# Down projection of a decoder layer: first operands in memory of their own, products 1, 6, 7 and 4 in one set of open banks, x brought into the result by transfers

## The chip, the cores and the metric

The kernel runs on one core of a Trainium2 chip. The metric is the device time of one execution in microseconds (us); lower is better. Inputs come from the chip's main memory and the result goes back there; on-chip work uses a large on-chip memory of 128 partitions, and a small accumulator memory of eight banks, each 128 x 512 float32, into which TensorE (PE) writes. VectorE (DVE) and ScalarE (ACT) do the elementwise work, GpSimd (POOL) a little, SyncE (SP) starts transfers (DMAs). Each engine works through its own list of instructions in order, and waits at an instruction until what it needs is there. A DMA that is started from an engine's list stands in that list like any other instruction.

## The reference

One decoder layer on 1024 tokens of width 1024: a SwiGLU feed-forward part, a token mixer (windowed attention and a gated delta rule), a second feed-forward part, a final norm. The change lies in the last matrix product of both feed-forward parts, the one with `w_down` (2816 x 1024).

```python
def swiglu(x, w_gate, w_up, w_down):
    return (jax.nn.silu(x @ w_gate) * (x @ w_up)) @ w_down

def reference(x, ...):
    for layer in range(DEPTH):           # DEPTH is 1
        x = x + 0.5 * swiglu(rmsnorm(x, ffn1_norm[layer]),
                             ffn1_w_gate[layer], ffn1_w_up[layer], ffn1_w_down[layer])
        h = rmsnorm(x, mix_norm[layer])
        x = x + hybrid_mixer(h, pos, w_in[layer], ...)
        x = x + 0.5 * swiglu(rmsnorm(x, ffn2_norm[layer]),
                             ffn2_w_gate[layer], ffn2_w_up[layer], ffn2_w_down[layer])
    return rmsnorm(x, final_norm)
```

## The kernel before

Float32 products are made from rounded halves. An operand v is split into H, which is v rounded (a CAST on ACT), and L = v - H (a subtraction on DVE); a product is the sum of three matmuls, H·H, L·H and H·L. Splitting one 128 x 512 block is therefore one ACT and one DVE instruction.

Both feed-forward parts use a 2 x 2 block scheme with seven block products in place of eight. The hidden part (`ff_hidden`, `ff_pair`) makes the activations for a pair of 128-wide blocks of the hidden width at a time, eleven pairs in all, and writes to memory, for each pair, seven combinations of them: the arrays `hd[0]` to `hd[6]` (in `order` rows `hd0_10` is `hd[0]` of pair 10). The write is `ff_left` (L259): a DMA that ACT starts. Three of the seven are activations themselves; the other four are sums that DVE makes in `ff_sums` (L264 to L271) at the end of a pair, each followed by its write. The tiles they are made in are called `e`; 14 of them take turns.

The down projection is `ff_down` (L451). It runs seven block products in the order 1, 5, 6, 7, 4, 3, 2. Each product n has eleven steps p, one for each pair: the left operand is `hd[n-1][p]`, loaded into a staging tile `st` (L461, seven tiles take turns) and split into `lH`, `lL`; the right operand is a block of `w_down`, or a combination of its blocks that DVE makes (tile `T`; two of the blocks are kept in the tiles `room`), and is split into `rH`, `rL`. A step then has 12 matmuls (L517): three for each of four banks. So a product has 132 matmuls. All loads are started by SP, in the order in which the program asks for them. The splits of the first two steps of product 1 (`head`) stand ahead of everything else of the projection.

The result is gathered in `acc` (1024 x 1024, in on-chip memory), in four quarters of four blocks each. Product 1 is in all four of them. Before the change, product 1 goes into the banks X, ACT writes half of it to the first quarter of `acc` (L531), x is loaded into eight tiles `xt` of 512 KB each (five take turns), and DVE makes the four starts "half of product 1 plus x" with 16 additions (L539 to L542). Product 5 is summed in other banks, Y; then X is opened anew for product 6, into which 7 and 4 are summed too. `add` (L524) adds half of a bank to a quarter of `acc`, one scalar_tensor_tensor on DVE for each block (L526).

The lines that matter:

```python
    X = [psum(C, tag) for tag in ("mm", "mm", "tC", "tC")]
    product(1, X, True)
    for t in range(4):
        nc.scalar.mul(quarter(0, 0, t), X[t], 0.5)
...
        tt(out=quarter(1, 1, t), in0=p1, in1=xs[0][:, 512:], op=ALU.add)
...
    product(5, Y, True)
    add(1, 1, Y)
    X = [psum(C, tag) for tag in ("mm", "mm", "tC", "tC")]
    product(6, X, True)
```

Memory is handed out in pools; a tile of the projection that lies where a tile of the hidden part lay must wait for the last use of that one. The order of instructions on each engine is set when the program is built, by a scheduler that goes by its own estimate of times.

Of the kernel before, what the change touches and what calls it, by code (L numbers as in the profile page):

```python
# [9 lines left out]
F32 = mybir.dt.float32  # L10
F32R = mybir.dt.float32r
I32 = mybir.dt.int32
AF = mybir.ActivationFunctionType
ALU = mybir.AluOpType
AX = mybir.AxisListType

P = 128
T = 1024
D = 1024
DFF = 2816  # L20
KT = D // P
NT = T // P
# [12 lines left out]
NPAIR = NF // 2  # L35
# [34 lines left out]
def psum(C, tag):  # L70
    return C.pp.tile([P, 512], F32, name=tag, tag=tag, bufs=BANKS[tag])
# [29 lines left out]
def rsqrt_cols(C, ssq, scale, eps, n, tag, pool=None):  # L101

    nc = C.nc
    pool = pool or C.tp
    v = pool.tile([P, n], F32, name=tag + "v", tag=tag + "v", bufs=4)
    y = pool.tile([P, n], F32, name=tag + "y", tag=tag + "y", bufs=4)
    t = pool.tile([P, n], F32, name=tag + "t", tag=tag + "t", bufs=4)
    nc.vector.tensor_scalar(v, ssq, scale, eps, op0=ALU.mult, op1=ALU.add)
    yi = y.bitcast(I32)
    nc.vector.tensor_scalar(yi, v.bitcast(I32), 1, -1, op0=ALU.logical_shift_right, op1=ALU.bitwise_xor)  # L110
    nc.vector.tensor_tensor(out=yi, in0=yi, in1=C.magic[:, :n], op=ALU.add)
    for _ in range(3):
        nc.vector.tensor_tensor(out=t, in0=y, in1=y, op=ALU.mult)
        nc.vector.scalar_tensor_tensor(t, t, -0.5, v, op0=ALU.mult, op1=ALU.mult)
        nc.vector.scalar_tensor_tensor(y, t, 1.5, y, op0=ALU.add, op1=ALU.mult)
    return y, v
# [136 lines left out]


def ff_e(C):
    return C.ep.tile([P, 512], F32, name="e", tag="e", bufs=14)


def ff_left(C, n, p, v):  # L259

    C.nc.scalar.dma_start(C.hd[n - 1][p], v)


def ff_sums(C, p, a11, a12, a21, a22):  # L264

    tt = C.nc.vector.tensor_tensor
    S = [ff_e(C) for _ in range(4)]
    tt(out=S[2], in0=a11, in1=a21, op=ALU.subtract)
    tt(out=S[0], in0=a21, in1=a22, op=ALU.add)
    tt(out=S[1], in0=S[0], in1=a11, op=ALU.subtract)  # L270
    tt(out=S[3], in0=a12, in1=S[1], op=ALU.subtract)  # L271
    for n, v in ((7, S[2]), (5, S[0]), (6, S[1]), (3, S[3])):
        ff_left(C, n, p, v)


def ff_plain(C, W, a, n=512):

    nc = C.nc
    acc = [(psum(C, "mm"), psum(C, "tC")) for _ in W]
    for n0 in range(0, 512, n):  # L280
        for wpair, pair in zip(W, acc):
            for halves, ps in zip(wpair, pair):
                c = slice(a * 512 + n0, a * 512 + n0 + n)
                for k in range(KT):
                    H, L = [v[:, k % 4 * P:k % 4 * P + P] for v in halves[k // 4]]
                    for i, (x, w) in enumerate(((C.hH, H), (C.hL, H), (C.hH, L))):
                        nc.tensor.matmul(ps[:, n0:n0 + n], w, x[:, k, c], start=k == 0 and i == 0, stop=k == KT - 1 and i == 2)  # L287
    out = []
    for pg, pu in acc:
        sg = ff_e(C)  # L290
        nc.scalar.activation(sg, pg, AF.Silu)
        nc.vector.tensor_tensor(out=sg, in0=sg, in1=pu, op=ALU.mult)
        out.append(sg)
    return out
# [156 lines left out]
def ff_down(C, x_dram, wd, early, late, between=None):  # L451

    nc = C.nc
    tt = nc.vector.tensor_tensor
    lead = []

    def stage(src):
        v = C.fp.tile([P, 512], F32, name="st", tag="st", bufs=7)[:, :src.shape[1]]  # L460
        lead.append(nc.sync.dma_start(v, src).ins)  # L461
        return v

    def load(v, src):
        with C.tc.issue_after(lead[11]):
            nc.sync.dma_start(v, src)

    def split(v, tag, bufs):
        out = [C.fp.tile([P, 512], F32R, name=tag + nm, tag=tag + nm, bufs=bufs) for nm in "HL"]
        n = v.shape[1]  # L470
        H, L = [o[:, :n] for o in out]
        nc.scalar.copy(H, v)  # L472
        tt(out=L, in0=v, in1=H.bitcast(F32), op=ALU.subtract)  # L473
        return H, L

    def block(p, k, c):
        r = (2 * p + k) * P
        return wd[r:r + P, c * 512:c * 512 + 512]


    B12, B22 = [C.hp.tile([P, 16, 512], F32, name="room", tag=nm, bufs=1) for nm in ("hH", "hL")]
    head = [(split(stage(C.hd[0][p]), "l", 6), split(stage(block(p, 0, 0)), "r", 8)) for p in range(2)]
    acc = C.fp.tile([P, NT, D], F32, name="acc")
    T = C.w0.tile([P, NPAIR, 512], F32, name="T", tag="T", bufs=1)
    T = [T[:, p] for p in range(NPAIR)]
    B12, B22 = [[b[:, p] for p in range(NPAIR)] for b in (B12, B22)]

    def right(n, p):
        if n == 1:
            return split(stage(block(p, 0, 0)), "r", 8)  # L490
        if n == 5:
            load(B12[p], block(p, 0, 1))
            tt(out=T[p], in0=B12[p], in1=stage(block(p, 0, 0)), op=ALU.subtract)
        elif n == 6:
            load(B22[p], block(p, 1, 1))
            tt(out=T[p], in0=B22[p], in1=T[p], op=ALU.subtract)
        elif n == 7:
            v = C.fp.tile([P, 512], F32, name="st", tag="st", bufs=7)
            tt(out=v, in0=B22[p], in1=B12[p], op=ALU.subtract)
            return split(v, "r", 8)  # L500
        elif n == 4:
            tt(out=T[p], in0=stage(block(p, 1, 0)), in1=T[p], op=ALU.subtract)
        v = (B22[p] if n == 3 else T[p]) if n != 2 else stage(block(p, 1, 0))
        return split(v, "r", 8)

    def product(n, banks, opens, ts=range(4)):
        c0, c1 = ts[0] * P, ts[-1] * P + P
        for p in range(NPAIR):
            if n == 1 and p < len(head):
                x, W = head[p]  # L510
            else:
                W = right(n, p)
                x = split(stage(C.hd[n - 1][p][:, c0:c1]), "l", 6)
            for t, ps in zip(ts, banks):
                m = slice(t * P - c0, t * P - c0 + P)
                for i, (a, b) in enumerate(((0, 0), (0, 1), (1, 0))):
                    nc.tensor.matmul(ps, x[a][:, m], W[b], start=opens and p == 0 and i == 0,  # L517
                                     stop=p == NPAIR - 1 and i == 2, skip_group_check=True)

    def quarter(r, c, t):  # L520
        return acc[:, r * 4 + t, c * 512:c * 512 + 512]

    def add(r, c, banks, ts=range(4)):
        for t, ps in zip(ts, banks):  # L524
            q = quarter(r, c, t)
            nc.vector.scalar_tensor_tensor(q, ps, 0.5, q, op0=ALU.mult, op1=ALU.add)  # L526

    X = [psum(C, tag) for tag in ("mm", "mm", "tC", "tC")]
    product(1, X, True)
    for t in range(4):  # L530
        nc.scalar.mul(quarter(0, 0, t), X[t], 0.5)  # L531
    for t in range(4):
        xs = []
        for r in (1, 0):
            xt = C.fp.tile([P, D], F32, name="xt", tag="xg", bufs=5)
            nc.sync.dma_start(xt, x_dram[(r * 4 + t) * P:(r * 4 + t) * P + P])
            xs.append(xt)
        p1 = quarter(0, 0, t)
        tt(out=quarter(1, 1, t), in0=p1, in1=xs[0][:, 512:], op=ALU.add)  # L539
        tt(out=quarter(1, 0, t), in0=p1, in1=xs[0][:, :512], op=ALU.add)  # L540
        tt(out=quarter(0, 1, t), in0=p1, in1=xs[1][:, 512:], op=ALU.add)
        tt(out=p1, in0=p1, in1=xs[1][:, :512], op=ALU.add)  # L542
    Y = [psum(C, tag) for tag in ("tA", "tA", "tM", "tM")]
    product(5, Y, True)
    add(1, 1, Y)
    X = [psum(C, tag) for tag in ("mm", "mm", "tC", "tC")]
    product(6, X, True)
    add(0, 1, X)
    product(7, X, False)
    add(1, 1, X)  # L550
    product(4, X, False)
    add(1, 0, X)
    product(3, Y, False)
    add(0, 1, Y)
    take_h(C)
    if between is not None:
        between()
    for t in range(4, 8):
        late([early(t, acc[:, t])])
    first = [early(t, acc[:, t]) for t in range(4)]  # L560
    for ts, tag in (((0, 1), "mm"), ((2, 3), "tC")):
        X = [psum(C, tag) for _ in ts]
        product(2, X, True, ts)
        add(0, 0, X, ts)
        late([first[t] for t in ts])


def consts(C, I):
# [939 lines left out]
def take_h(C):  # L1508
    C.hH, C.hL = [C.hp.tile([P, KT, T], F32R, name=nm, tag=nm, bufs=1) for nm in ("hH", "hL")]
# [118 lines left out]
```

## Time and profile before

| what | us |
|---|---|
| median of 3 runs | 2587.6 |
| lowest and highest of them | 2586.91, 2592.05 |
| the profiled execution, its own time | 2586.69 |
| its span in the profile | 2585.0 |
| first down projection in the span | about 462 to 690 |
| second down projection in the span | about 2351 to 2585 |

The profile gives each instruction's start and duration, and for an engine's idle time the event that ended it. Matmuls overlap: one that is listed with 0.39 us is followed by the next after about 0.23 us, so that times between starts, not durations, tell how long a row of them took. "PEclk" is the share of full speed that TensorE was granted.

### The profile page before, as it was taken

How to read it: one execution, taken by the hardware profiler on the slowest of the kernel's cores; microseconds unless marked ns; L12 is line 12 of the kernel's file. 1: busy time of each engine (PE TensorE's matmuls, PEld its weight loads, DVE VectorE, ACT ScalarE, POOL GpSimd, SP SyncE). 2: the span in 40 equal slices, each digit the busy share in tenths (PEclk: the TensorE clock that was granted, in tenths of full speed). 3: DMA queues.
4: the chain of work that ended last, by engine and by line, in shares of the span. 5: the costliest groups of instructions: out<-in, count | busy, mean ns of one | idle time of the engine just before them, and what ended most of it. 6: DMA issues, size and time to landing. Idle time of an engine off the chain costs nothing.

```text
span 2585.0 us, 35524 instructions
## 1 busy us (share of the span) xinstructions
PE 2504.2 (97%) x12835; PEld 2085.1 (81%) x12835; DVE 1756.3 (68%) x4032; ACT 1042.7 (40%) x1900; POOL 97.3 (4%) x96
## 2 busy tenths in 40 slices
PE   7899999899999999999999999999998999999998
PEld 7788888688888877888888888887877888887786
DVE  6966665697634447688887777356557766665977
ACT  4433332355533346444434343254343333333445
POOL 0000000000110010000000000001010000000000
PEclk9999999999999999999999999999999999999999
DMA  4233232765533332222223223265431323325656
GB/s 156 82 106 110 90 106 90 276 226 163 175 85 84 94 77 71 67 71 76 65 65 88 56 64 92 72 214 181 155 131 57 118 90 106 110 91 211 231 150 193
DMA packets 272176, 306.74 MB, mean 119 GB/s; under 512 B 43040, under 2 KB 188160, under 8 KB 272000
## 3 DMA queue, kind: packets, MB, share of 16 engines
q1 hardware_dynamic: 249824, 264.10, 32.9%
q10 hardware_dynamic: 22176, 40.38, 4.2%
q8 instruction: 101, 1.65, 0.3%
q14 instruction: 75, 0.61, 0.1%
HBM read 224.09 MB, written 74.02 MB: 115 GB/s over the span
## 4 chain that ended last, share of the span: by engine, by line
PE 87%; DVE 5%; DMA 4%; ACT 2%; issue 1%; SPq 0%; ACTq 0%; DVEq 0%
PE mm L82 28%; PE tC L388 12%; PE mm L388 8%; PE tM L388 8%; PE mm L517 6%; PE tC L517 5%; PE tC L82 4%; PE tA L82 2%; PE tA L517 2%; PE tM L517 2%; PE mm L287 2%; PE tC L287 2%; PE tM L82 1%; PE tA L86 1%; PE tC L1496 1%; DMA sgl<-sgbd 1%
## 5 line engine op out<-in xcount | busy, mean ns | idle before, releaser
L82 PE MATMUL mm<-hH,wL 128*128 128x512 f32 x960 | 384.9, 401 | 0.0
L82 PE MATMUL mm<-hH,wH 128*128 128x512 f32 x960 | 383.6, 400 | 0.0
L82 PE MATMUL mm<-hL,wH 128*128 128x512 f32 x960 | 380.9, 397 | 0.0
L236 ACT CAST fH<-fraw 128x512 fp32r<-128x512 f32 x256 | 156.0, 620 | 383.9 <-PE tC L388 68.6
L237 DVE TENSOR_TENSOR fL<-fraw,fH 128x512 fp32r<-128x512 f32 x256 | 173.5, 685 | 72.4 <-ACT fH L236 71.2
L82 PEld LDWEIGHTS mm<-hL,wH 128*128 128x128 f32 x960 | 181.1, 189 | 34.9
L82 PEld LDWEIGHTS mm<-hH,wL 128*128 128x128 f32 x960 | 180.9, 188 | 34.8
L82 PEld LDWEIGHTS mm<-hH,wH 128*128 128x128 f32 x960 | 181.1, 189 | 32.8
L472 ACT CAST lH<-st 128x512 fp32r<-128x512 f32 (+1 forms) x176 | 99.6, 566 | 153.4 <-issue 64.5
L133 DVE TENSOR_TENSOR wL<-wraw,wH 128x1024 fp32r<-128x1024 f32 x94 | 116.6, 1240 | 64.1 <-ACT wH L132 63.8
L473 DVE TENSOR_TENSOR lL<-st,lH 128x512 fp32r<-128x512 f32 (+1 forms) x176 | 113.1, 643 | 50.1 <-ACT lH L472 47.2
L132 ACT CAST wH<-wraw 128x1024 fp32r<-128x1024 f32 x94 | 98.4, 1049 | 115.6 <-PE mm L82 63.7
L388 PE MATMUL mm<-hH,fH 128*128 128x512 f32 x320 | 125.2, 391 | 0.0
L388 PE MATMUL mm<-hL,fH 128*128 128x512 f32 x320 | 125.0, 391 | 0.0
L388 PE MATMUL mm<-hH,fL 128*128 128x512 f32 x320 | 124.8, 390 | 0.0
L790 DVE CUSTOM_DVE_ANT_0 s<-tC,masks 128x128 f32<-128x128 f32 (+1 forms) x96 | 30.1, 348 | 103.0 <-PE tC L82 68.9
L517 PE MATMUL mm<-rH,lH 128*128 128x512 f32 x220 | 87.3, 397 | 12.0 <-ACT rH L472 12.0
L517 PE MATMUL mm<-rL,lH 128*128 128x512 f32 x220 | 87.5, 398 | 0.0
L517 PE MATMUL mm<-rH,lL 128*128 128x512 f32 x220 | 86.7, 394 | 0.0
L517 PE MATMUL tC<-rH,lH 128*128 128x512 f32 x220 | 86.4, 393 | 0.0
L517 PE MATMUL tC<-rH,lL 128*128 128x512 f32 x220 | 86.4, 393 | 0.0
L517 PE MATMUL tC<-rL,lH 128*128 128x512 f32 x220 | 86.3, 392 | 0.0
(426 smaller groups left out, 6214.4 us busy)
## 6 DMA issues: line engine op xcount, KB each, us to landing
hd<-e ACTq DMA_DIRECT2D x154, 256.0 KB, 2.0
st<-hd SPq DMA_DIRECT2D x132, 256.0 KB, 3.4
wraw<-in_w_in_dram SPq DMA_DIRECT2D x64, 512.0 KB, 4.0
st<-in_ffn_w_down_dram SPq DMA_DIRECT2D x110, 256.0 KB, 3.5
fraw<-in_ffn_w_gate_dram SPq DMA_DIRECT2D x22, 1024.0 KB, 5.4
fraw<-in_ffn_w_up_dram SPq DMA_DIRECT2D x22, 1024.0 KB, 5.9
room<-in_ffn_w_down_dram SPq DMA_DIRECT2D x44, 256.0 KB, 5.5
wraw<-in_w_branch_b_dram SPq DMA_DIRECT2D x16, 512.0 KB, 4.3
```

The source lines that it names most:

```text
L82: pin(C, C.nc.tensor.matmul(*args, **kw))
L86: pin(C, C.nc.tensor.transpose(out, in_, C.ident if ident is None else ident))
L132: nc.scalar.copy(H[:, :width], raw[:, :width])
L133: nc.vector.tensor_tensor(out=L[:, :width], in0=raw[:, :width], in1=H[:, :width].bitcast(F32), op=ALU.subtract)
L236: nc.scalar.copy(h, src)
L237: nc.vector.tensor_tensor(out=l, in0=src, in1=h.bitcast(F32), op=ALU.subtract)
L287: nc.tensor.matmul(ps[:, n0:n0 + n], w, x[:, k, c], start=k == 0 and i == 0, stop=k == KT - 1 and i == 2)
L388: nc.tensor.matmul(ps, w, x[:, k], start=opens and k == 0 and q == 0, stop=k == 3 and q == 2, skip_group_check=True)
L472: nc.scalar.copy(H, v)
L473: tt(out=L, in0=v, in1=H.bitcast(F32), op=ALU.subtract)
L517: nc.tensor.matmul(ps, x[a][:, m], W[b], start=opens and p == 0 and i == 0, stop=p == NPAIR - 1 and i == 2, skip_group_check=True)
L790: nc.vector.tensor_tensor_reduce(s[:, h, :nk], ps[h][:, :nk], mask, 1.0, NEG, op0=ALU.add, op1=ALU.max, accum_out=o[:, 128 + h:129 + h])
```

## The change

In both feed-forward parts alike:

- The splits of the first two steps of product 1 get memory of their own: eight slots of one tile `first`, in the place that `T` takes later, on the other side of memory. The staging tiles `st` stay where they were. To make room, the `e` tiles go from 14 to 13, and three small tiles of the norms from 4 to 3.
- The seven writes of the last pair (p = 10) to `hd` are started by SP, no longer by ACT.
- x is loaded straight into `acc` (eight DMAs of 512 KB). The ACT multiplications and the 16 DVE additions go; `add(0, 0, X)` adds half of product 1 to the first quarter.
- Product 6 does not open new banks: it is summed on top of product 1 in X, and so are 7 and 4. The three other quarters thus get product 1 with their own `add`.

```diff
 def ff_e(C):
-    return C.ep.tile([P, 512], F32, name="e", tag="e", bufs=14)
+    return C.ep.tile([P, 512], F32, name="e", tag="e", bufs=13)
...
 def ff_left(C, n, p, v):
-    C.nc.scalar.dma_start(C.hd[n - 1][p], v)
+    eng = C.nc.sync if p == NPAIR - 1 else C.nc.scalar
+    eng.dma_start(C.hd[n - 1][p], v)
...
-    def split(v, tag, bufs):
-        out = [C.fp.tile([P, 512], F32R, name=tag + nm, tag=tag + nm, bufs=bufs) for nm in "HL"]
+    def split(v, tag, bufs, out=None):
+        out = out or [C.fp.tile([P, 512], F32R, name=tag + nm, tag=tag + nm, bufs=bufs) for nm in "HL"]
...
-    head = [(split(stage(C.hd[0][p]), "l", 6), split(stage(block(p, 0, 0)), "r", 8)) for p in range(2)]
+    first = C.w0.tile([P, NPAIR, 512], F32R, name="first", tag="T", bufs=1)
+    slots = [[first[:, 3 + 2 * i], first[:, 4 + 2 * i]] for i in range(4)]
+    head = [(split(stage(C.hd[0][p]), "l", 6, slots[2 * p]), split(stage(block(p, 0, 0)), "r", 8, slots[2 * p + 1])) for p in range(2)]
...
     product(1, X, True)
-    for t in range(4):
-        nc.scalar.mul(quarter(0, 0, t), X[t], 0.5)
-    for t in range(4):
-        xs = []
-        for r in (1, 0):
-            xt = C.fp.tile([P, D], F32, name="xt", tag="xg", bufs=5)
-            nc.sync.dma_start(xt, x_dram[(r * 4 + t) * P:(r * 4 + t) * P + P])
-            xs.append(xt)
-        p1 = quarter(0, 0, t)
-        tt(out=quarter(1, 1, t), in0=p1, in1=xs[0][:, 512:], op=ALU.add)
-        tt(out=quarter(1, 0, t), in0=p1, in1=xs[0][:, :512], op=ALU.add)
-        tt(out=quarter(0, 1, t), in0=p1, in1=xs[1][:, 512:], op=ALU.add)
-        tt(out=p1, in0=p1, in1=xs[1][:, :512], op=ALU.add)
+    for t in range(NT):
+        load(acc[:, t], x_dram[t * P:t * P + P])
+    add(0, 0, X)
     Y = [psum(C, tag) for tag in ("tA", "tA", "tM", "tM")]
     product(5, Y, True)
     add(1, 1, Y)
-    X = [psum(C, tag) for tag in ("mm", "mm", "tC", "tC")]
-    product(6, X, True)
+    product(6, X, False)
```

Two places show what this does to the engines' lists; the first projection is shown, and the second reads the same. The first place is the end of the hidden part. SP's list there, before, from the last load of the hidden part (`fraw`) on: the stage loads of product 1 stand right behind it.

```order
L245 DMA fraw_3550<-in_ffn1_w_up_dram 128x8x256
L461 DMA st_3847<-hd0_0_73 128x512
L461 DMA st_3853<-in_ffn1_w_down_dram 128x512
L461 DMA st_3859<-hd0_1_74 128x512
L461 DMA st_3865<-in_ffn1_w_down_dram 128x512
L461 DMA st_3901<-in_ffn1_w_down_dram 128x512
```

SP's list at the same place after the change:

```order
L245 DMA fraw_3550<-in_ffn1_w_up_dram 128x8x256
L262 DMA hd3_10_116<-e_3716 128x512
L262 DMA hd0_10_83<-e_3749 128x512
L262 DMA hd1_10_94<-e_3631 128x512
L262 DMA hd6_10_149<-e_3824 128x512
L262 DMA hd4_10_127<-e_3822 128x512
L262 DMA hd5_10_138<-e_3823 128x512
L262 DMA hd2_10_105<-e_3825 128x512
L462 DMA st_3848<-hd0_0_73 128x512
L462 DMA st_3852<-in_ffn1_w_down_dram 128x512
L462 DMA st_3856<-hd0_1_74 128x512
L462 DMA st_3860<-in_ffn1_w_down_dram 128x512
```

The seven writes of pair 10 now stand ahead of the stage loads on SP; the last four of them wait for the sums that DVE makes last. ACT's list at that place, as a piece of the difference, from the last activation of pair 10 on, is rid of them:

```order
L261 DMA hd6_10_149<-e_3824 128x512
L261 DMA hd4_10_127<-e_3822 128x512
L261 DMA hd5_10_138<-e_3823 128x512
L261 DMA hd2_10_105<-e_3825 128x512
L472 CAST lH_3849<-st_3847 128x512
L472 CAST rH_3855<-st_3853 128x512
```

That was ACT before; after the change the casts follow on the activation at once:

```order
L418 ACTIVATE e_3631<-e_3631 128x512
L375 ACTIVATE e_3661<-e_3661 128x512
L473 CAST first_3847<-st_3848 128x512
L473 CAST first_3847<-st_3852 128x512
L473 CAST first_3847<-st_3856 128x512
```

On DVE nothing moves there: the four sums (L268 to L271, after the change L269 to L272) stand ahead of the first four subtractions of the splits in both.

The second place is the passage from product 1 to product 5. DVE's list before, from the first combination `T` of product 5 on (rows of the third step of product 5, `rL_4214` and `lL_4220`, stand among the 16 additions):

```order
L493 TENSOR_TENSOR T_3872<-room_3845,st_4210 128x512
L539 TENSOR_TENSOR acc_3871<-acc_3871,xt_4121 128x512
L540 TENSOR_TENSOR acc_3871<-acc_3871,xt_4121 128x512
L541 TENSOR_TENSOR acc_3871<-acc_3871,xt_4123 128x512
L539 TENSOR_TENSOR acc_3871<-acc_3871,xt_4129 128x512
L542 TENSOR_TENSOR acc_3871<-acc_3871,xt_4123 128x512
L540 TENSOR_TENSOR acc_3871<-acc_3871,xt_4129 128x512
L541 TENSOR_TENSOR acc_3871<-acc_3871,xt_4131 128x512
L539 TENSOR_TENSOR acc_3871<-acc_3871,xt_4137 128x512
L542 TENSOR_TENSOR acc_3871<-acc_3871,xt_4131 128x512
L540 TENSOR_TENSOR acc_3871<-acc_3871,xt_4137 128x512
L541 TENSOR_TENSOR acc_3871<-acc_3871,xt_4139 128x512
```

DVE's list there after the change:

```order
L497 TENSOR_TENSOR T_3865<-room_3845,st_4127 128x512
L530 SCALAR_TENSOR_TENSOR acc_3864<-mm_3866,acc_3864 128x512
L530 SCALAR_TENSOR_TENSOR acc_3864<-mm_3867,acc_3864 128x512
L530 SCALAR_TENSOR_TENSOR acc_3864<-tC_3868,acc_3864 128x512
L530 SCALAR_TENSOR_TENSOR acc_3864<-tC_3869,acc_3864 128x512
L474 TENSOR_TENSOR rL_4131<-T_3865,rH_4130 128x512
L474 TENSOR_TENSOR lL_4137<-st_4134,lH_4136 128x512
L497 TENSOR_TENSOR T_3865<-room_3845,st_4153 128x512
L474 TENSOR_TENSOR lL_4163<-st_4160,lH_4162 128x512
L497 TENSOR_TENSOR T_3865<-room_3845,st_4179 128x512
L474 TENSOR_TENSOR rL_4157<-T_3865,rH_4156 128x512
```

Four additions from the banks stand in place of 16, but now ahead of the splits of product 5's very first step (before, the first two steps' splits were done by then, and the third's stood among the additions). On SP the loads of x stand in both between the last stage load of product 1 and the first load of product 5; five stood there before, with three more among the loads of product 5, and now all eight do:

```order
L462 DMA st_4092<-hd0_10_83 128x512
L467 DMA acc_3864<-in_x_dram 128x1024 x8
L467 DMA room_3845<-in_ffn1_w_down_dram 128x512
L462 DMA st_4127<-in_ffn1_w_down_dram 128x512
L462 DMA st_4134<-hd4_0_117 128x512
```

More of the change, by code (lines that the diff above doesn't have):

```diff
@@ L104, in rsqrt_cols @@
     pool = pool or C.tp
-    v = pool.tile([P, n], F32, name=tag + "v", tag=tag + "v", bufs=4)
-    y = pool.tile([P, n], F32, name=tag + "y", tag=tag + "y", bufs=4)
-    t = pool.tile([P, n], F32, name=tag + "t", tag=tag + "t", bufs=4)
+    v = pool.tile([P, n], F32, name=tag + "v", tag=tag + "v", bufs=3)
+    y = pool.tile([P, n], F32, name=tag + "y", tag=tag + "y", bufs=3)
+    t = pool.tile([P, n], F32, name=tag + "t", tag=tag + "t", bufs=3)
     nc.vector.tensor_scalar(v, ssq, scale, eps, op0=ALU.mult, op1=ALU.add)
@@ L559, in ff_down @@
         late([early(t, acc[:, t])])
-    first = [early(t, acc[:, t]) for t in range(4)]
+    begun = [early(t, acc[:, t]) for t in range(4)]
     for ts, tag in (((0, 1), "mm"), ((2, 3), "tC")):
@@ L564, in ff_down @@
         add(0, 0, X, ts)
-        late([first[t] for t in ts])
+        late([begun[t] for t in ts])
 def consts(C, I):
```

## The prediction

> **What bounds the kernel.** I read the page first, then what PE waited for in the two stretches that the change touches, then the timelines of PE, ACT, DVE and SP at those places.
>
> ```profile
> span 2585.0 us, 35524 instructions
> PE 2504.2 (97%) x12835; PEld 2085.1 (81%) x12835; DVE 1756.3 (68%) x4032; ACT 1042.7 (40%) x1900; POOL 97.3 (4%) x96
> ```
>
> PE is busy for 2504.2 of 2585.0 us. The change alters no matmul, so only PE's idle or slow time can change: 80.8 us in the whole kernel, and what lies in the two projections is this (PE's waits, summed, first for the first projection, then for the second):
>
> ```profile
> PE mm L517 <- ACT rH L472: 6.0, 1, 6.0
> PE tA L517 <- DVE lL L473: 1.6, 1, 1.6
> PE tA L517 <- ACT rH L472: 0.7, 1, 0.7
> ...
> PE mm L517 <- ACT rH L472: 6.0, 1, 6.0
> PE tA L517 <- DVE lL L473: 2.8, 1, 2.8
> ```
>
> Each projection has one wait of 6.0 us at its first matmul, and a second place, in product 5 (banks tA). Everything else of the two projections either runs without waits or is not touched. The timeline of PE gives both places their full size, with the slow clock in them:
>
> ```profile
> 461.75 0.39 PE L388 MATMUL tM<-hH,fL 128*128 128x512 f32 x1
> 468.11 0.79 PE L517 MATMUL mm<-rH,lH 128*128 128x512 f32 x1 [5.97 <-ACT rH L472]
> 472.48 0.39 PE L517 MATMUL tC<-rH,lH 128*128 128x512 f32 x1
> 500.37 0.39 PE L517 MATMUL tA<-rH,lH 128*128 128x512 f32 x1
> 533.54 0.39 PE L517 MATMUL mm<-rH,lH 128*128 128x512 f32 x1
> ...
> 2356.82 0.79 PE L517 MATMUL mm<-rH,lH 128*128 128x512 f32 x1 [5.98 <-ACT rH L472]
> 2363.62 0.39 PE L517 MATMUL mm<-rH,lH 128*128 128x512 f32 x1
> 2390.16 0.39 PE L517 MATMUL tA<-rH,lH 128*128 128x512 f32 x1
> 2425.22 0.39 PE L517 MATMUL mm<-rH,lH 128*128 128x512 f32 x1
> ```
>
> Product 1 has 132 matmuls. Nine of them start before 472.48; the other 123 take until 500.37, so 0.2267 us each at full clock, 29.92 us for a product. The first nine took 4.37 us instead of 2.04: 2.33 us lost to the clock (and to rL, which came a little late). In the second projection 15 took 6.80 us instead of 3.40: 3.40 lost. Product 5 runs from its first tA to the next mm: 33.17 us, 3.25 too many; in the second projection 35.06, 5.14 too many, of which a slow clock is a part. By stages (columns: window, its length, busy time of PE, of its weight loads, DVE, ACT, POOL, then the granted clock, DMA share and GB/s) the clock was full in the first projection's product 5, and 0.66 in five us of the second's:
>
> ```profile
> 500.00:530.00 30.00, 27.76 (x120) 21.85 (x119) 29.79 (x50) 14.88 (x27) 0.00 (x0) 1.00 0.93 330
> ...
> 2400.00:2405.00 5.00, 4.34 (x11) 2.99 (x12) 5.00 (x9) 2.30 (x4) 0.00 (x0) 0.66 0.63 196
> ```
>
> So the most that the change could win is about 2 x 6.1 + 2.33 + 3.40 at the starts and 3.25 + 5.14 in product 5, 26 us or 1.0%. Now what it really takes away.
>
> **The start of the projection.** These are ACT, DVE and SP around it:
>
> ```profile
> 464.42 2.40 ACTq L261 DMA_DIRECT2D hd<-e  x4
> 466.92 0.62 ACT L472 CAST lH<-st 128x512 fp32r<-128x512 f32 x1 [6.10 <-DVE e L271]
> 467.44 0.61 ACT L472 CAST rH<-st 128x512 fp32r<-128x512 f32 x1
> ...
> 465.75 0.69 DVE L271 TENSOR_TENSOR e<-e 128x512 f32<-128x512 f32 x1
> 468.18 0.68 DVE L473 TENSOR_TENSOR rL<-st,rH 128x512 fp32r<-128x512 f32 x1
> ...
> 460.29 6.50 SPq L461 DMA_DIRECT2D st<-in_ffn_w_down_dram  x2
> 470.75 0.38 SPq L461 DMA_DIRECT2D st<-in_ffn_w_down_dram  x1
> 471.22 0.38 SPq L461 DMA_DIRECT2D st<-hd  x1
> ```
>
> The staged data had long landed; the first cast stood on ACT behind four DMA issues, each of which waited for one of the four sums, the last of which ended at 465.75 + 0.69 = 466.44. After the change ACT is free of them, and `first` waits for no old tile. But SP's list shows the four writes there now, ahead of all stage loads, with the same wait for the same sums. The last write is issued at about 466.5 for 0.33 us; the first stage load follows at about 466.9 and the second 0.47 later (the spacing of the last two SP rows), at 467.35. How long such a load takes, from issue to landing, in five short windows:
>
> ```profile
> st<-hd SPq DMA_DIRECT2D x1, 256.0 KB, 2.6
> hd<-e ACTq DMA_DIRECT2D x1, 256.0 KB, 2.0
> ...
> st<-in_ffn_w_down_dram SPq DMA_DIRECT2D x1, 256.0 KB, 3.5
> hd<-e ACTq DMA_DIRECT2D x1, 256.0 KB, 3.8
> ...
> st<-hd SPq DMA_DIRECT2D x1, 256.0 KB, 5.0
> ```
>
> 2.6 us is a load alone, 3.5 the load that SP issued at 460.29 + 6.50 - 0.33 = 466.46 beside the last write, 5.0 one of the later loads in the row. The second load, which carries rH, lands between 467.35 + 2.6 = 469.95 and 467.35 + 5.0 = 472.35; I take 3.0, nearer to the load beside one write than to the full row: 470.35. Then the cast, 0.62, and PE 0.08 later (468.11 against 467.44 + 0.61 gives 0.06): **471.05 in place of 468.11, 2.9 us later** in each projection. The stage loads lose a cover that the page does not name as a cost: before, four of them were issued ahead of the end of the hidden part. From below: were the loads there in time all the same, the gain would be small, because DVE's list still has the four sums ahead of lL and rL. rL would end at 466.44 + 0.6 + 0.69 = 467.8 where it ended at 468.86 before, and the second matmul needs it. So the start moves by -1.1 to +4.9, and I take +2.9, twice: **+5.9**.
>
> For the clock I take no change. Both waits were 5.97 and 5.98 us long, yet cost 2.33 and 3.40, so the loss does not go by the wait's length in these two rows. The Trainium skill, "TensorE: Matmul & The Clock Gate", section "What's actually happening", says why that may be so: the clock is halved after an idle window of 3.4 us, and the windows run freely, so a start lands anywhere in one; these two rows agree (both waits are longer than one window, the slow stretches of 4.37 and 6.80 us both end within two). By that rule a wait of 9 us costs no more clock than one of 6; were the loss to grow in proportion, the sum would be 2.9 higher.
>
> **Product 1 to product 5.** Before, DVE did the additions of x first, and the splits of step 3 came late behind them (in the second projection also behind a late `xt`):
>
> ```profile
> L539 DVE TENSOR_TENSOR acc<-acc,xt x8: 681/684/693, 499.2 to 2397.9; 128x512 f32<-128x512 f32 x8
> ...
> 505.79 0.68 DVE L473 TENSOR_TENSOR rL<-T,rH 128x512 fp32r<-128x512 f32 x1
> 508.80 0.68 DVE L473 TENSOR_TENSOR lL<-st,lH 128x512 fp32r<-128x512 f32 x1
> ...
> L526 DVE SCALAR_TENSOR_TENSOR acc<-mm,acc x16: 678/682/684, 562.0 to 2563.6; 128x512 f32<-128x512 f32 x16
> ```
>
> That goes: 16 x 0.68 = 10.9 us of DVE become 4 x 0.68 = 2.7. What is late next: the four new additions wait for the banks of product 1, the last of them for its last matmul, and rL and lL of product 5's first step stand behind. With 0 at the end of product 1: the last addition ends at about 0.2 + 0.68 = 0.9, rL at 1.6, lL at 2.2. PE can run the four H·H matmuls until 0.9 and then waits 0.7; the second step's T, rH and rL follow and are some 0.3 late. From there DVE needs three instructions for a step, 3 x 0.6 to 0.69 = 1.8 to 2.1 us, against PE's 2.72, and catches up. So about 1.0 us is left of 3.25 and of 5.14; too short for a slow clock, since the stalls of up to 1.6 us in the first projection left it at full speed. That is **-2.25 and -4.14, together -6.4**; the bounds are -8.4 (no stall at all) and 0 (another stall of the same size).
>
> This needs the operands to be there. Before:
>
> ```profile
> 480.96 2.70 SPq L536 DMA_DIRECT2D xt<-in_x_dram  x5
> 484.44 0.48 SPq L461 DMA_DIRECT2D st<-in_ffn_w_down_dram  x1
> 493.26 0.69 DVE L493 TENSOR_TENSOR T<-room,st 128x512 f32<-128x512 f32 x1 [6.42 <-DMA st<-in_ffn_w_down_dram]
> ...
> 462.00:475.00 13.00, 7.01 (x22) 5.21 (x22) 9.56 (x15) 5.29 (x10) 0.00 (x0) 0.74 0.70 229
> 475.00:500.00 25.00, 25.00 (x112) 20.72 (x111) 14.54 (x23) 11.85 (x20) 0.00 (x0) 1.00 0.99 359
> ```
>
> The first T came at 493.26, 7 us ahead of its use at 500.37. After, product 1 ends near 471.05 + 29.92 + 2.5 for the clock = 503.5, and up to that T there are 22 stage loads, all eight loads of x and two blocks to move: 22 x 0.262 + 8 x 0.524 + 2 x 0.262 = 10.5 MB. At the 359 GB/s of the full stretch that is 29.2 us after about 468.2 (first data of the first load), so 497.4; T, rH and lH need 1.4 more, 498.8. The cover is 4.7 us, and it is gone if the transfers run below 10.5 MB in 33.9 us, 310 GB/s. Taking the four ACT multiplications away (0.6 us each) gives nothing, since ACT is not waited for there. Opening no new banks gives nothing either: X's additions are done 30 us before product 6.
>
> The rest costs nothing by the lists: with 13 `e` tiles the waits for a finished write move to a tile one earlier, and a tile comes round again only after more than one pair (38 us, 168 matmuls of 0.2267), against 2.0 us for a write; the norms' small tiles are few at a time. The start of the mixer has some waits in other places since memory is laid out anew; its loads already waited for the same writes of x one to three rows later. I give these together -1 to +1.
>
> **The sum.** +5.9 - 6.4 = -0.5 against the profiled execution's own time of 2586.69, so 2586.2. The median of the three runs, 2587.6, is 0.9 above that execution; against the median the forecast is 2587.1, and I say 2587.0. About 0.2% (5.2 us) is what a measurement of this kernel can tell from no change; the three runs before are 5.1 apart.
>
> **Rivals.**
> (a) Faster: the stage loads are not held by the writes (SP's order does not bind, or the loads land within 466.5 in some other way). For it: the change gives the casts memory of their own, which only pays if data is there. Against it: in this trace SP issues in list order: the load of 466.46 came 0.04 after the write issued at 464.42 had landed, and everything behind it came later. The starts would then win 1.1 each: -2.2 - 6.4 = -8.6, 2579. A milder form (rH at 469.95, product 5 without a stall, both starts at the short end of the clock's loss) gives +5.1 - 8.4 - 1.6 = -4.9, at the edge of faster.
> (b) Slower: transfers are the new limit of product 5. Place: the eight loads of x ahead of its first T. Price: at 270 GB/s, between the two stretches' 229 and 359, the first T comes at 468.2 + 38.9 = 507.1, lH and rH at 508.5, 5.0 late; then 0.786 MB a step take 2.91 us against 2.72, 1.9 more over ten steps, and one slow stretch of 3.4 us costs 1.7: 8.6 a projection in place of 3.25 and 5.14, so +8.8 + 5.9 = +14.7, 2602. It decides from about 290 GB/s downward. Against it: whenever loads stood in line, the rate was near 359.
> (c) Slower, without a new limit: the head's loads take 5.0 us as the late ones of the row did, +9.8, and product 5 keeps half its stall, -3.2: +6.6, 2594.
> (d) The change does not do what it says at the start: that is in the forecast, since memory of their own frees the casts of a wait that SP's list brings back.
>
> **How the numbers follow.** The forecast, terms within the bounds above but not all at one end, has 0.62 and by itself covers 2582 to 2593: +4 to +8 at the starts, -8 to -4 in product 5, 1.6 for the clock either way. (a) with its milder form has 0.19, (b) 0.08, (c) 0.11. The range leaves out half of (a) and of (c) and most of (b): 2580.5 to 2595. Faster by over 0.2%: 0.19. Within 0.2%: 0.62. Slower by over 0.2%: 0.19.
>
> **What would show each step.** The first cast of the projection ends its wait on a DMA of `st`, not on a sum, and PE starts about 9 us after the hidden part's last matmul instead of 6.4; the first stage load on SP is issued right after the last `hd` write. Product 5, from its first tA to the next mm, takes 30 to 31.5 us in both projections, with a wait on rL in its first step. DMA stays near 0.99 from the first load of x to product 5. The forecast is wrong if PE starts earlier than 6.4 us after its last matmul, if product 5 waits for a DMA, or if PE waits anywhere in the hidden part or at the mixer's start where it did not before.

## The result and the profile after

| | before | changed |
|---|---|---|
| median of 6 runs each, us | 2588.18 | 2611.26 |
| lowest and highest, us | 2583.78, 2592.05 | 2608.62, 2614.35 |
| span of the profiled execution, us | 2585.0 | 2607.8 |

The changed kernel takes 1.0088 of the time before (95% interval 1.0077 to 1.0099): 23 us slower, far outside the range. The page of the changed kernel gives its span, then the busy time of each engine:

```profile
span 2607.8 us, 35507 instructions
PE 2527.1 (97%) x12835; PEld 2082.0 (80%) x12835; DVE 1745.4 (67%) x4008; ACT 1039.1 (40%) x1892; POOL 98.0 (4%) x96
```

PE was busy for 2504.2 us and is now busy for 2527.1, with the same 12835 matmuls: 22.9 us, all of the loss. Its idle time is 80.7 us (2607.8 less 2527.1), where it was 80.8. So PE does not wait more in sum; its matmuls take longer. A lower granted clock would show in the mean of the whole run, and this is 0.988 in both. What did the two places of the prediction do? PE's timeline at the first projection, then at the second (the last matmul of the hidden part, then the first of the projection, of product 5 and of product 6):

```profile
467.33 0.40 PE L389 MATMUL tM<-hH,fL 128*128 128x512 f32 x1
476.88 3.23 PE L521 MATMUL mm<-first 128*128 128x512 f32 x6 [9.15 <-ACT first L473]
...
509.15 0.62 PE L521 MATMUL tA<-rH,lH 128*128 128x512 f32 x2
...
540.16 0.39 PE L521 MATMUL mm<-rH,lH 128*128 128x512 f32 x1
...
2374.65 0.40 PE L389 MATMUL tM<-hH,fL 128*128 128x512 f32 x1
2384.63 3.23 PE L521 MATMUL mm<-first 128*128 128x512 f32 x6 [9.59 <-ACT first L473]
...
2417.03 0.62 PE L521 MATMUL tA<-rH,lH 128*128 128x512 f32 x2
...
2448.02 0.39 PE L521 MATMUL mm<-rH,lH 128*128 128x512 f32 x1
```

PE starts 9.55 and 9.98 us after the hidden part's last matmul (476.88 against 467.33, 2384.63 against 2374.65) instead of 6.36 and 6.37, and product 5 takes 31.01 and 30.99 us instead of 33.17 and 35.06. Both are near what the prediction said. But the last matmul of the hidden part itself, which the change does not touch, starts at 467.33 instead of 461.75: 5.58 us were lost before the projection began. Two windows in the middle of the first hidden part, of before and of the changed kernel (busy time and number of PE's matmuls, then weight loads, DVE, ACT, POOL, the granted clock, DMA share, GB/s):

```profile
200.00:300.00 100.00, 100.00 (x443) 82.81 (x442) 65.31 (x106) 32.04 (x53) 0.00 (x0) 1.00 0.33 112
```

```profile
200.00:300.00 100.00, 100.00 (x436) 81.46 (x435) 64.49 (x105) 30.87 (x51) 0.00 (x0) 1.00 0.33 111
```

PE waits for nothing in either, the clock is full, the DMA share the same, yet 436 matmuls fit where 443 did: 1.6% fewer. The groups of instructions of PE, shapes kept apart, tell which ones (moving tile first, then the weight tile; count, busy us, mean ns of one). Before:

```profile
L82 PE MATMUL mm<-hH,wL 128*128 128x512 f32 x960 | 384.9, 401 | 0.0
...
L388 PE MATMUL tM<-hH,fH 128*128 128x512 f32 x160 | 62.2, 389 | 0.0
...
L388 PE MATMUL tM<-t1H,fH 128*128 128x512 f32 x160 | 62.2, 389 | 0.0
...
L388 PE MATMUL tC<-t3H,fH 128*128 128x512 f32 x160 | 62.2, 389 | 0.0
```

and in the changed kernel:

```profile
L82 PE MATMUL mm<-hH,wL 128*128 128x512 f32 x960 | 388.1, 404 | 0.0
...
L389 PE MATMUL tM<-hH,fH 128*128 128x512 f32 x160 | 63.2, 395 | 0.0
...
L389 PE MATMUL tM<-t1H,fH 128*128 128x512 f32 x160 | 62.2, 389 | 0.0
...
L389 PE MATMUL tC<-t3H,fH 128*128 128x512 f32 x160 | 62.2, 389 | 0.0
```

The matmuls that stream `hH` or `hL` take 6 ns longer in the hidden parts and in the mixer's L157 (tC<-hH,wH 395 in place of 389), and 3 ns on the mean in the mixer's L82; those that stream the sums `t1` and `t3`, past the same weights, take what they took. The spacing says the same: these start one after another here,

```profile
299.93 0.39 PE L389 MATMUL mm<-hH,fH 128*128 128x512 f32 x1
...
303.89 0.40 PE L389 MATMUL tC<-hH,fL 128*128 128x512 f32 x1
```

with 17 intervals between the two rows, so 0.2329 us each against the 0.2267 at full pace. Summed over its groups, `hH` and `hL` cost 6.1 us more in the hidden parts' groups of the banks mm (381.1 against 375.0), 5.9 in those of tC and tM (379.3 against 373.4), 9.5 in L82 (1158.9 against 1149.4) and 2.4 in L157 (152.1 against 149.7): 23.9 us, against the 22.9 by which all of PE's busy time grew.

What differs for them? The edits make three small tiles of the norms shorter (`rsqrt_cols`, 4 buffers to 3). They are made under three tags, so nine buffers of 32 bytes go, and every tile of the hidden parts that the build places behind them starts 288 bytes lower. In the built program `hH` stands ahead of them, at byte 960 of a partition in both kernels, and `hL` 32768 behind it; the first `fH` moves from 88256 to 87968, and `t1H` from 125120 to 124832, with it. So `hH` has another place against the weights, `t1` has not. That is theory 1: a matmul is slower when moving tile and weight tile do not start at the same place within some unit of bytes.

### The profile page after: what moved, and what is told of

The parts are those of the page before. It is cut to its first block, busy times and chain, and to the rows that moved or that the text cites. A ratio compares the mean times of both kernels' runs of the same rounds, so it can differ in the third digit from the quotient of the medians.

```text
span 2607.8 us, 35507 instructions
## 1 busy us (share of the span) xinstructions
PE 2527.1 (97%) x12835; PEld 2082.0 (80%) x12835; DVE 1745.4 (67%) x4008; ACT 1039.1 (40%) x1892; POOL 98.0 (4%) x96
## 4 chain that ended last, share of the span: by engine, by line
PE 89%; DVE 4%; DMA 3%; ACT 2%; issue 1%; SPq 0%; DVEq 0%; ACTq 0%
PE mm L82 28%; PE tC L389 12%; PE mm L389 8%; PE tM L389 8%; PE tC L521 5%; PE mm L521 5%; PE tC L82 3%; PE tA L82 2%; PE tA L521 2%; PE tM L521 2%; PE mm L288 2%; PE tC L157 2%; PE tC L288 2%; PE mm L157 2%; PE tM L82 1%; PE tA L86 1%
## 5 line engine op out<-in xcount | busy, mean ns | idle before, releaser
L82 PE MATMUL mm<-hH,wL 128*128 128x512 f32 x960 | 388.1, 404 | 0.0
L82 PE MATMUL mm<-hH,wH 128*128 128x512 f32 x960 | 386.9, 403 | 0.0
L82 PE MATMUL mm<-hL,wH 128*128 128x512 f32 x960 | 383.9, 400 | 0.0
L82 PEld LDWEIGHTS mm<-hH,wL 128*128 128x128 f32 x960 | 180.8, 188 | 37.9
L82 PEld LDWEIGHTS mm<-hL,wH 128*128 128x128 f32 x960 | 180.9, 188 | 37.6
L82 PEld LDWEIGHTS mm<-hH,wH 128*128 128x128 f32 x960 | 181.0, 189 | 35.4
```

The costliest lines, as they stand in the source:

```text
L82: pin(C, C.nc.tensor.matmul(*args, **kw))
```

## The experiments

**The norms' tiles alone, and a pad.** Theory 2 says that the weights' own place counts, theory 3 that it is the order, the tiles `e` or `first`. Four kernels, the first from before, the second and third from the changed kernel, the fourth from before:

```diff
# e1_norm3 (before)
-    v = pool.tile([P, n], F32, name=tag + "v", tag=tag + "v", bufs=4)
+    v = pool.tile([P, n], F32, name=tag + "v", tag=tag + "v", bufs=3)
...
# e2_after_pad (changed)
-    ssq = C.tp.tile([P, 1], F32, name="ssq", tag="ssq", bufs=4)
+    ssq = C.tp.tile([P, 1], F32, name="ssq", tag="ssq", bufs=5)
# e3_after_shift_h (changed), e4_before_shift (before)
-    C.magic = C.cp.tile([P, 16], I32, name="magic")
+    C.magic = C.cp.tile([P, 24], I32, name="magic")
```

> The kernel before, with nothing changed but the three small tiles of the norms from 4 buffers to 3 (nine buffers of 32 bytes: every tile that lies behind them starts 288 bytes lower, hH and hL lie ahead of them and stay at 960 and 33728). Theory 1 (relative place): a matmul is slower when its moving tile and its weight tile start 32 bytes apart within 64 bytes; here hH and hL stay at 0 within 64, the weight tiles fH, fL, wH, wL go to 32: 19 to 24 us slower than before, 2607 to 2612, with 395 to 398 ns for the groups mm, tC, tM <- hH/hL, fH/fL and 389 for t1H, t3H. Theory 2 (absolute place: weights that don't start on a 64-byte boundary load slower beside hH): the same time. Theory 3 (the slower pace comes from the new order, from the 13 tiles e or from the tile first): within 2 us of before, 2588, all groups as before.

> The changed kernel with one more 32-byte buffer (tile ssq, 5 instead of 4) behind the norms' small tiles, so that all tiles behind start 32 bytes higher, at 0 within 64 as hH does. Theories 1 and 2: the pace comes back, 20 to 24 us faster than the changed kernel, 2587 to 2591, groups of hH at 389 to 391 ns. Theory 3: 2611, no change.

> The changed kernel with the 32 bytes added ahead of hH (tile magic, 24 instead of 16 columns): hH and hL go to 32 within 64, the weights and t1 to t3 to 0. Theory 1: the two are 32 apart as in the changed kernel, so it stays within 3 us of 2611, hH groups 395 to 398, t1H and t3H 389. Theory 2: the weights are on a 64-byte boundary again, so 2587 to 2591. Theory 3: 2611.

> The kernel before with the same 32 bytes ahead of hH (magic, 24 columns): everything, hH, weights and t1 to t3, moves to 32 within 64, together. Theory 1: no change, within 2 us of 2588, all groups at 389 to 391. Theory 2: the weights are off the boundary, so about 20 us or more slower. Theory 3: no change.

Measured, with later runs on the same question (distance: start of the first `fH` minus that of `hH`, and of `t1H` minus `fH`, as remainders by 256; ns: groups tM<-hH,fH and tM<-t1H,fH; ratio to before on the same chip):

| kernel | fH - hH | t1H - fH | ns hH | ns t1H | median us | ratio (95%) |
|---|---|---|---|---|---|---|
| before | 0 | 0 | 389 | 389 | | |
| changed | 224 | 0 | 395 | 389 | 2611.26 | 1.0088 (1.0077 to 1.0099) |
| e1_norm3 | 224 | 0 | 395 | 389 | 2607.98 | 1.0083 (1.0061 to 1.0104) |
| e2_after_pad | 0 | 0 | 389 | 389 | 2586.65 | 0.9991 (0.9982 to 1.0001) |
| e3_after_shift_h | 224 | 0 | 395 | 389 | 2610.5 | 1.0085 (1.0069 to 1.0101) |
| e4_before_shift | 0 | 0 | 389 | 389 | 2589.41 | 1.0007 (0.9998 to 1.0016) |
| i1_before_64 | 64 | 0 | 394 | 389 | 2604.92 | 1.0066 (1.005 to 1.0082) |
| j1_before_128 | 128 | 0 | 395 | 389 | 2607.86 | 1.0076 (1.0059 to 1.0094) |
| j2_before_t_off | 0 | 32 | 389 | 395 | 2598.27 | 1.0036 (1.0023 to 1.005) |

Before with the three bufs alone loses 19.7 us (2607.98 against the 2588.29 of before beside it), about what the whole change loses, and 32 bytes of pad give it back. Theory 3 falls with both. Theory 2 falls with the third and fourth: `e3_after_shift_h` has the weights back on a multiple of 64 and stays slow; `e4_before_shift` has them off it and is not slower. Of the three, only the distance sets the slow kernels apart from the others.

**The unit.** The expectations went by 64 bytes. Two more buffers, and four more, behind the norms' tiles of before:

```diff
-    ssq = C.tp.tile([P, 1], F32, name="ssq", tag="ssq", bufs=4)
# i1_before_64
+    ssq = C.tp.tile([P, 1], F32, name="ssq", tag="ssq", bufs=6)
# j1_before_128
+    ssq = C.tp.tile([P, 1], F32, name="ssq", tag="ssq", bufs=8)
```

> The kernel before with two more 32-byte buffers of ssq behind the norms' tiles: all tiles behind them start 64 bytes higher, so hH stands at 64 and the weights at 0 within 128 bytes, both at 0 within 64. Theory 1 with 64 bytes as the unit: within 2 us of before, 2588, hH groups at 389 to 391. Theory 1 with 128 bytes as the unit: as slow as the changed kernel or more, 2608 and up, hH groups at 395 or more.

> The kernel before with four more 32-byte buffers of ssq: all tiles behind the norms' start 128 bytes higher, hH stays. 64 bytes apart was slow (i1_before_64), so the unit is not 64. With 128 as the unit hH and the weights start at the same place again: within 2 us of before, 2588, hH groups 389 to 391. With 256 as the unit they are 128 apart: slow as the changed kernel, 2605 to 2612, hH groups 394 to 398. (256 apart within 512 is what the kernel before has.)

Both are slow, so neither 64 nor 128 bytes is the unit. `i1_before_64` stayed 3 us under the 2608 that was named as the least, with its groups at 394; whether 64 bytes cost a little less than 128, the two intervals don't tell. The group of the second, 128 bytes off:

```profile
L388 PE MATMUL tM<-hH,fH 128*128 128x512 f32 x160 | 63.2, 395 | 0.0
...
L388 PE MATMUL tM<-t1H,fH 128*128 128x512 f32 x160 | 62.2, 389 | 0.0
```

256 fits every row of the table. 512 does not: the distance is 87296 in the kernel before, 341 times 256, and 87040 in `e2_after_pad`, 340 times 256; these are 256 apart, and both run at 389 ns. Of distances that are no multiple of 256, only 32, 64, 128 and 224 were run.

**Another operand.** If it is a matter of any two tiles, the sums `t1` to `t3` must suffer when they alone are moved:

```diff
# j2_before_t_off (before, in ff_hidden)
+        C.nc.vector.memset(C.tb.tile([P, 8], F32, name="pad"), 0.0)
```

> The kernel before with a pad of 32 bytes ahead of t1 to t3 alone (one memset more in each hidden part): hH, hL and the weights stay together, the sums t1, t2, t3 (and the tiles e behind them) are 32 bytes off the weights. Theory 1: now the groups of t1H, t1L, t3H, t3L go to 395 and those of hH, hL stay at 389 to 391; 480 matmuls of each of t1, t2, t3 by 6 ns are 8.6 us: 2595 to 2598. Rival (the place matters for hH and hL only, the largest tiles, or the norms' tiles count in another way): all groups as before, 2588.

The groups change places, here one of each:

```profile
L388 PE MATMUL tM<-t1H,fH 128*128 128x512 f32 x160 | 63.2, 395 | 0.0
...
L388 PE MATMUL tM<-hH,fH 128*128 128x512 f32 x160 | 62.2, 389 | 0.0
```

The loss is 10.6 us (2598.27 against 2587.67), and the 8.6 of 1440 matmuls by 6 ns lies inside its interval (0.23 to 0.50%, 6 to 13 us).

**The parts of the change, at the old pace.** `e2_after_pad` is the change with its memory mended, and it takes the time before. Each of its two parts alone:

```diff
# h1_x_alone (before): first, writes, e and the norms' tiles stay as they were
-    for t in range(4):
-        nc.scalar.mul(quarter(0, 0, t), X[t], 0.5)
...
+    for t in range(NT):
+        load(acc[:, t], x_dram[t * P:t * P + P])
+    add(0, 0, X)
...
-    X = [psum(C, tag) for tag in ("mm", "mm", "tC", "tC")]
-    product(6, X, True)
+    product(6, X, False)
# h2_start_alone (e2_after_pad): the same lines put back
```

> The kernel before with the part on x and the products alone: the eight loads of x into the result, product 6 into the open banks; first, the writes, the tiles e and the norms' tiles as before. Theory 1: product 5 goes from 33.2 and 35.1 to about 31.0 in both projections, the starts stay at 6.4 us, all groups of hH at 389 to 391: 6 us faster than before, about 2582. Rival (x loads or the open banks cost as much elsewhere in the projection): within 2 us of before.

> The padded changed kernel with the part on x and the products put back as before: first, the writes on SP, the 13 tiles e and the norms' three tiles stay. It has the later start alone: both starts 9.5 us after the hidden part's last matmul instead of 6.4, so 5 to 7 us slower than before, 2593 to 2595; product 5 as before or worse, 33 to 36 us. Rival (the later start is caught up in product 1 or 5): within 2 us of before.

`h1_x_alone`: 2581.16 us, ratio 0.9977 (0.9966 to 0.9987), 6.4 us less than the 2587.51 of before beside it. Its product 5 (first and second projection):

```profile
501.30 0.73 PE L517 MATMUL tA<-rH,lH 128*128 128x512 f32 x2 [0.23 <-ACT lH L472]
...
532.58 0.39 PE L517 MATMUL mm<-rH,lH 128*128 128x512 f32 x1
...
2388.43 0.62 PE L517 MATMUL tA<-rH,lH 128*128 128x512 f32 x2
...
2419.41 0.39 PE L517 MATMUL mm<-rH,lH 128*128 128x512 f32 x1
```

31.28 and 30.98 us. `h2_start_alone`: 2592.9 us, ratio 1.0017 (1.0008 to 1.0027), 5.2 us more, just under what was expected; PE starts 9.59 and 9.40 us after the hidden part's last matmul. Its product 5 is 33.21 us in the first projection, as before, but 33.38 in the second, where before had 35.06. So the change holds a gain of 6 us and a loss of 5 that nearly cancel, and a third effect of 23 that is in neither part.

**The start.** What holds it is tested on the padded kernel, with the last pair's writes on other queues:

```diff
-    eng = C.nc.sync if p == NPAIR - 1 else C.nc.scalar
# g1_writes_act
+    eng = C.nc.scalar
# g2_writes_pool
+    eng = C.nc.gpsimd if p == NPAIR - 1 else C.nc.scalar
```

> The padded changed kernel (e2_after_pad) with the last pair's seven hd writes back on ACT; the casts into first keep memory of their own. Theory 1 (SP's list order holds the start: loads stand behind the writes): the loads are early again, the casts wait behind the four writes on ACT as before, PE starts 6.3 to 6.5 us after the hidden part's last matmul instead of 9.5, so 6 to 7 us less than e2_after_pad: 2579 to 2581. Rival (something other than SP's order holds the loads or the casts, such as the memory of first or of st): the gap stays at 9.5, 2586.

> The padded changed kernel with the last pair's seven hd writes on POOL, so that neither SP nor ACT waits for the sums. Theory 1: the loads are early, the first casts run on ACT right after its last work, rL and lL wait only for DVE's sums; PE starts 3.5 to 5.5 us after the hidden part's last matmul, 1 to 3 us a projection less than with the writes on ACT: 2575 to 2579. Rival (the memory of the stage tiles or of first is free only at the end of the hidden part): as with the writes on ACT or later, 2580 and more.

`g1_writes_act`: 2582.41 us, ratio 0.9977 (0.9967 to 0.9988). The gap is 6.30 us in both projections, as expected, and the time is 1.4 us above the forecast. So memory of their own for the first operands gains next to nothing while ACT starts the writes: before, the gap was 6.36 and 6.37. `g2_writes_pool`: 2579.83 us, ratio 0.9974 (0.9963 to 0.9984), 0.8 above. Its start, on PE and on DVE:

```profile
462.72 0.39 PE L389 MATMUL tM<-hH,fL 128*128 128x512 f32 x1
462.95 0.42 PE L521 MATMUL mm<-first 128*128 128x512 f32 x1
468.67 1.65 PE L521 MATMUL mm<-first 128*128 128x512 f32 x3 [5.31 <-DVE first L474]
```

```profile
466.73 0.69 DVE L272 TENSOR_TENSOR e<-e 128x512 f32<-128x512 f32 x1
467.33 2.49 DVE L474 TENSOR_TENSOR first<-st,first 128x512 fp32r<-128x512 f32 x4
```

The first matmul of the projection follows the hidden part's last without a gap, which I had put at 3.5 to 5.5 us; then PE waits 5.31 us for the second operand, since DVE's list has the four sums ahead of it. The bound has gone from SP's list to DVE's. `h1_x_alone`, `g1_writes_act` and `g2_writes_pool` are all faster than both kernels, by 0.23 to 0.26% than before; among themselves the intervals don't part them. `h1_x_alone` is the smallest edit of the three.

## Why the prediction was wrong

Its own terms, against the two profiled executions of before and changed:

| term | predicted | measured | from |
|---|---|---|---|
| two starts | +5.9 | +6.8 | 9.55 and 9.98 us of gap in place of 6.36 and 6.37 |
| clock in product 1 | 0 | -0.9 | 32.27 and 32.40 us in place of 32.26 and 33.34 |
| product 5 | -6.4 | -6.2 | 31.01 and 30.99 in place of 33.17 and 35.06 |
| rest | -1 to +1 | +23.2 | what is left of 22.8 |

**The step that failed** is the last: "The rest costs nothing by the lists." It rests on the premise of the first paragraph, "The change alters no matmul, so only PE's idle or slow time can change". The runs showed a third way: idle time (80.8 and 80.7 us) and granted clock (0.988) stayed, and the same 12835 matmuls were busy for 22.9 us more, since each that streams `hH` or `hL` past weights at another remainder took 3 to 6 ns longer. The prediction touched the cause in passing ("since memory is laid out anew") and priced it as waits in other places, because only waits and orders were asked of the lists. The lists show no addresses, and the profile of before shows `hH` and `t1H` at the same 389 ns, so nothing in it gave the price of an address. But the places could have been looked at: the build's places of `hH` and `fH` were there, and the one edit that moved one against the other took 288 bytes, a multiple of 32 and of no higher power of two. No rival held it either: all four were about the two projections, and the time was lost outside them, 5.6 us of it before the first began. Nor could its signs of being wrong have caught it: they are an early start, a wait for a DMA, and new waits. Shown by runs: `e1_norm3` (this edit alone has the loss), `e2_after_pad` (its 32 bytes alone take it back).

**The start** held, 0.9 us short in sum. SP issues the first stage load right behind the writes, and the cast waits for that load. DVE's timeline in the changed kernel with the last sum, then SP's, then ACT's:

```profile
471.35 0.69 DVE L272 TENSOR_TENSOR e<-e 128x512 f32<-128x512 f32 x1
```

```profile
463.68 8.70 SPq L262 DMA_DIRECT2D hd<-e  x5
472.48 0.41 SPq L462 DMA_DIRECT2D st<-hd  x1
473.01 0.37 SPq L462 DMA_DIRECT2D st<-in_ffn_w_down_dram  x1
```

```profile
475.53 1.30 ACT L473 CAST first<-st 128x512 fp32r<-128x512 f32 x2 [9.20 <-DMA st<-hd]
```

The last sum ended at 471.35 + 0.69 = 472.04, so the load follows by 0.44, where 0.46 was forecast, and the second by 0.53 instead of 0.47. The first lands about 3.0 us after its issue, and both casts are done at 476.83, 0.05 ahead of PE. Most of the 0.9 lies in the second projection: there the second load was issued at 2380.29 and its cast began at 2383.96, 3.7 us later, where 3.0 had been taken. Rival (a), that SP's order does not bind, is refuted by these rows and by `g1_writes_act`, which takes the gap back. Two waits of over 9 us cost the clock 2.35 and 2.48 us of product 1 (its length less the 29.92 of full pace), those of 6 us had cost 2.34 and 3.42: no growth with the length, as the prediction had assumed. It had taken that from the Trainium skill, "TensorE: Matmul & The Clock Gate", section "What's actually happening", by which the clock is halved after one idle window of about 3.4 us; these four waits agree.

**Product 5** held within 0.1 us of its working in each projection. The stall is at the place that was named, an operand's low half behind the new additions (PE's timeline of the changed kernel):

```profile
510.70 0.74 PE L521 MATMUL tA<-rL,lH 128*128 128x512 f32 x2 [0.48 <-DVE rL L474]
```

Transfers did not become the limit (rival b). The window of the 29 us ahead of product 5 in the changed kernel has the DMA share and the rate at its end, and DVE's timeline the first T:

```profile
480.00:509.00 29.00, 29.00 (x127) 23.90 (x126) 14.26 (x22) 12.10 (x20) 0.00 (x0) 0.98 0.99 359
```

```profile
505.61 0.69 DVE L497 TENSOR_TENSOR T<-room,st 128x512 f32<-128x512 f32 x1 [11.13 <-DMA st<-in_ffn_w_down_dram]
```

The share is 0.99 at 359 GB/s, and T was begun 3.5 us ahead of its product's first matmul (505.61, 509.15), where 6.1 had been worked out (497.4, 503.5): less cover, but enough.

**The sum without the failed term** held: the padded kernel takes 2586.65 us, and the forecast was 2587.0. But it is the time of another kernel than the one that was forecast. Some luck is in it: in the changed kernel the starts came out 0.9 us over their term and the clock 0.9 under, and the clock's loss had differed by 1.1 us between the two starts of before, at the same wait.

## What to carry to other kernels

When an edit changes the number or size of any tile, small ones too, compare where the build puts the tiles that TensorE streams and those it loads as weights, before and after; nine small buffers fewer in a helper cost about 20 us here (`e1_norm3`). When PE's busy time changes and its count does not, group its matmuls by operand and compare the mean of one: here all groups of one operand had moved and those of another had not, past the same weights. Judge a change's parts at the old layout (a pad is enough), or a gain of 6 us is hidden behind something that belongs to neither part.

## What the hardware showed that was not expected

In the hidden parts' 128 x 512 float32 matmuls, a moving tile and a weight tile whose starts differ by a multiple of 256 bytes ran at 389 ns (0.2267 us from start to start); with 32, 64, 128 or 224 bytes more, at 394 to 395 (0.2329 with 224), at full clock and with weight loads of 0.19 us in both. In the mixer's L82 the difference was 3 ns on the mean, in its L157 again 6. It went the other way for some matmuls of 256 columns: the group tC<-hH,fL, 128x256, took 285 ns before, 282 in the changed kernel and 285 with the pad. The same shape in the banks mm tells nothing: mm<-hH,fH ran at 293 to 302 ns among the kernels whose tiles stand together.

```profile
L288 PE MATMUL tC<-hH,fL 128*128 128x256 f32 x64 | 18.0, 282 | 0.0
```

What in the chip does this stays open: whether the moving tile meets its own weights or the next ones, which are loaded while it streams, no run here tells, since all weights of a row of matmuls stand at the same remainder. The products of the projection, whose two tiles stayed together in every run, were not tried apart.
